# Down-projection's first 40 k-tiles by one level of Strassen's algorithm, in four chunks

## The chip, the core and the metric

The kernel runs on one core of a Trainium2 chip. Its engines run side by side and wait for each other through semaphores: TensorE (PE: matmuls into PSUM), VectorE (DVE), ScalarE (ACT), GpSimd (POOL) and SyncE (SP), whose queue issues nearly all transfers between HBM and SBUF. The metric is the device time of one execution, in microseconds.

## The reference, cut to the part that matters

One layer: token mixers, then a gated feed-forward network, then a residual and a final norm. The part at hand is the last third:

```
def conv_ffn(h, st, w_up, ffn_conv_w, ffn_conv_b, w_down):
    gate, val = jnp.split(h @ w_up, 2, axis=-1)
    gate_c, new_st = causal_dwconv(gate, st, ffn_conv_w)
    act = jax.nn.silu(gate_c + ffn_conv_b) * val
    return act @ w_down, new_st
...
        f, s_f = conv_ffn(h, ffn_s[l], w_up[l], ffn_conv_w[l], ffn_conv_b[l], w_down[l])
        x = x + g2 * f
...
    y = rmsnorm(x, final_norm)
```

There are 576 positions (512 of the prompt, 64 of the sample), 2048 model columns and 5632 hidden columns, all float32.

## The kernel before

Everything is held transposed: features on the 128 partitions, positions along the free dimension in two halves of 288 (256 prompt, 32 sample). With P = 128 the hidden size is 44 tiles (NFF), the model size 16 (KD).

Float32 precision comes from two-part operands. Each operand is split into a high part (a rounded copy, made by ScalarE) and a low part (the difference, by VectorE), and a product is three matmuls: high x high, high x low, low x high. Weights are split as they arrive (`up_split`, `wtile`), activations once.

The up stage (`up`, `up_prep`, `up_product`, `up_out`) already uses one level of Strassen's algorithm in Winograd's form. A unit is one hidden tile t. Its four weight blocks a11, a21, a22, a12 (8 k-tiles of 128 columns each) are loaded by `up_load` into six raw buffers; VectorE makes four sums of them; seven products of 8 x 3 matmuls on 290 columns follow, each against a combination of the activations that was made once and stays in SBUF (`combos[c, j]`, 7 x 8 slots). The combinations' order is B11, T1, T2, B21, T3, B22, T4. Three PSUM banks per unit gather the products. A product's weights are split two steps ahead (`ahead = 2`; three buffers each for high and low parts). The gate's convolution and the activation (`up_conv`, `up_act`) of unit t-1 are done while unit t runs, and the result goes to HBM as `actd[t]`.

The down stage (`down`) takes the hidden tiles in groups of four. `acts(g)` loads four tiles of `actd` and splits them, one group ahead. For each of the 16 output tiles, `mm6` does the six matmuls of each k-tile (three products, two halves of 288 columns), and `residual` multiplies by the gate and adds onto `x1[m]`, which was reloaded from `xd[m]`. The slots for all that are the up stage's combinations, which are no longer needed.

The last group of four k-tiles is in `final`, together with the transposition back, the final norm and the stores.

The program's text is not the order of execution: a list scheduler orders each engine's instructions by priority and by when it expects their operands. Once ordered, an engine runs its instructions in order, and so does SyncE with the transfers that it issues.

Of the kernel before, what the change touches and what calls it, by code (L numbers as in the profile page):

```python
# [16 lines left out]
P = 128  # L17
# [23 lines left out]
N_HRAW = 9  # L41
N_RAW = 6
NW = 66
OFF_AQ, OFF_AK, OFF_AV, OFF_AR, OFF_ALR = 0, 512, 1024, 2048, 3072
# [55 lines left out]
class Kern:  # L100
# [633 lines left out]
    def raw_late(self):  # L734

        pool, tag = self.raws[self.n_raw % N_RAW]
        self.n_raw += 1
        return pool.tile([P, 1024], F32, tag=tag, name=self.name("raw"))

# [767 lines left out]
    def parts(self, j):  # L1507
        lo, hi = self.x1[j], self.x1[j + NPAIR]
        return lo[:, 0], lo[:, 1], hi[:, 0], hi[:, 1]
# [96 lines left out]
    def up_load(self, t, names):  # L1606
        for n in names:
            raw = self.raw_late().rearrange("p (k n) -> p k n", k=NPAIR)
            row, half = {"a11": (0, 0), "a12": (0, 1), "a21": (1, 0), "a22": (1, 1)}[n]
            self.nc.sync.dma_start(raw, self.w_cols("w_up", row * NFF + t, half * NPAIR)(0, NPAIR))  # L1610
            self.a[t, n] = raw

    def up_split(self, src):
        hi, lo = [self.wq.tile([P, 1024], F32R, tag="w" + c, bufs=3, name=self.name("w" + c))
                  .rearrange("p (k n) -> p k n", k=NPAIR) for c in "hl"]
        self.nc.scalar.activation(hi, src, AF.Copy)  # L1616
        self.nc.vector.tensor_tensor(lo, src, hi.bitcast(F32), op=ALU.subtract)  # L1617
        self.split_of = self.nc.cur_bb.bb.instructions[-1]
        return hi, lo

    def up_s(self, c):
        return self.ua.tile([P, NPAIR, P], F32, tag=f"s{c}", name=self.name("s"))

    def up_first(self, t):

        s1 = self.a[t, "s1"] = self.up_s(1)
        self.nc.vector.tensor_tensor(s1, self.a[t, "a21"], self.a[t, "a22"], op=ALU.add)  # L1627

    def up_prep(self, t, c):

        V, a = self.nc.vector, self.a
        g = lambda n: a[t, n]
        if c == 0:
            w = self.up_split(g("a11"))
            with self.tc.issue_after(self.split_of):
                self.up_first(t)
        elif c == 1:
            w = self.up_split(g("s1"))
            s2 = a[t, "s2"] = self.up_s(2)
            with self.tc.issue_after(self.split_of):  # L1640
                V.tensor_tensor(s2, g("s1"), g("a11"), op=ALU.subtract)
        elif c == 2:
            w = self.up_split(g("s2"))
            if t + 1 < NFF:
                self.up_load(t + 1, ("a11", "a21"))
        elif c == 3:
            w = self.up_split(g("a12"))
        elif c == 4:
            V.tensor_tensor(g("a21"), g("a11"), g("a21"), op=ALU.subtract)
            w = self.up_split(g("a21"))  # L1650
            if t + 1 < NFF:
                self.up_load(t + 1, ("a22", "a12"))
        elif c == 5:
            V.tensor_tensor(g("s2"), g("a12"), g("s2"), op=ALU.subtract)
            w = self.up_split(g("s2"))
        else:
            w = self.up_split(g("a22"))
        a[t, "w", c] = w

    def up_product(self, t, c):  # L1660

        if c == 0:
            self.banks = [self.bank()[:, :HZ] for _ in range(3)]
        T, (wh, wl) = self.nc.tensor, self.a.pop((t, "w", c))
        ps = self.banks[(0, 2, 1, 0, 1, 2, 1)[c]]
        for j in range(NPAIR):
            hi, lo, _ = self.combos[c, j]

            T.matmul(ps, wh[:, j], hi, start=(c < 3 and j == 0), stop=False, skip_group_check=True)  # L1669
            T.matmul(ps, wh[:, j], lo, start=False, stop=False, skip_group_check=True)  # L1670
            T.matmul(ps, wl[:, j], hi, start=False, stop=(j == NPAIR - 1), skip_group_check=True)  # L1671

    def up_out(self, t, c):

        nc = self.nc
        V, A, G = nc.vector, nc.scalar, nc.gpsimd
        x, y, z = self.banks
        tmp = lambda n: self.ub.tile([P, HZ], F32, tag=n, name=self.name(n))
# [50 lines left out]
    def up_begin(self):  # L1729

        self.a, self.n_raw = {}, 0
        self.up_load(0, ("a11", "a21", "a22", "a12"))

    def up(self):
# [3 lines left out]
        self.up_state(0)  # L1738
        self.t2s = {}
        ahead = 2  # L1740
        steps = [(t, c) for t in range(NFF) for c in range(7)]
        for n, (t, c) in enumerate(steps):
            if t == 0:
                for l in ((1,), (2,), (3,), (4,), (5, 6), (), ())[c]:
                    for j in range(N_EARLY, NPAIR):
                        self.pair_late(l, j)
            if n + ahead < len(steps):
                self.up_prep(*steps[n + ahead])
            self.up_product(t, c)
            if n == 0:  # L1750
                norm = self.norm_end()
            if n < 2:
                next(norm, None)

            if t > 0 and c == 0:
                with self.tc.issue_after(self.split_of):
                    self.up_conv(t - 1, self.ca)
                self.up_state(t)
            if t > 0 and c == 2:
                with self.tc.issue_after(self.split_of):  # L1760
                    self.up_act(t - 1, self.v, self.ca)
            self.up_out(t, c)
        self.up_conv(t, self.ca)
        self.up_act(t, self.v, self.ca)


    def acts(self, g):

        nc, out = self.nc, []
        places = self.sets[g % 2]  # L1770
        for n in range(4):
            raw, hh, hl = [self.slot(places[3 * n + i], (F32, F32R, F32R)[i], HT) for i in range(3)]
            nc.sync.dma_start(raw, self.actd[4 * g + n])
            nc.scalar.activation(hh, raw, AF.Copy)
            nc.vector.tensor_tensor(hl, raw, hh.bitcast(F32), op=ALU.subtract)
            out.append((hh, hl))
        return out

    def down(self):
        free = [self.combos[c, j][2] for c in range(7) for j in range(NPAIR)]  # L1780
        take = lambda n: [free.pop(0) for _ in range(n)]
        self.sets = [take(12), None]
        acts = self.acts(0)
        self.raw = self.raw_late
        places = take(KD)
        self.sets[1] = take(12)
        for m in range(KD):
            self.x1[m] = self.slot(places[m], F32)
            self.nc.sync.dma_start(self.x1[m], self.xd[m])
        for g in range(NFF // 4 - 1):  # L1790
            for m0 in range(0, KD, 2):
                wh, wl = self.wtile(self.w_down(4 * g, m0))
                if m0 == 6:
                    ahead = self.acts(g + 1)
                for m in range(m0, m0 + 2):
                    ps = self.pgt()
                    c = slice((m - m0) * P, (m - m0 + 1) * P)
                    for k in range(4):
                        self.mm6(ps, wh[:, k, c], wl[:, k, c], acts[k], k == 0, k == 3)
                    self.residual(ps, self.x1[m], self.mod[:, 5, m])  # L1800
            acts = ahead
        g = NFF // 4 - 1
        self.final(acts, free + self.sets[(g + 1) % 2] + self.sets[g % 2][0::3])

# [5 lines left out]
    def final(self, acts, free):  # L1810
# [10 lines left out]
        for h in range(2):  # L1821
# [3 lines left out]
            for m in range(KD):  # L1825
# [4 lines left out]
                for k in range(4):  # L1830
                    self.mm6(ps, w[m][0][:, k], w[m][1][:, k], acts[k], k == 0, k == 3, ((h, HT),), m % 2)
                self.residual(ps[:, m % 2:m % 2 + 1], self.x1[m][:, h:h + 1], self.mod[:, 5, m])
                if late and m % 4 == LATE:
# [39 lines left out]
    def final_part(self, h, q, blocks):  # L1873
# [3 lines left out]
        for c0, n, y, ms in blocks:  # L1877
            ps = self.bank()
            z0 = c0 if c0 < HP else ZS
            for j in range(4):  # L1880
                T.transpose(ps[:n, j * P:(j + 1) * P], self.x1[4 * q + j][:, h, z0:z0 + n], self.c["ident"])
            junk = self.v_tile().rearrange("p h t -> p (h t)")
# [22 lines left out]
def layer_kernel(tc, i, o):  # L1905
    nc = tc.nc
    with ExitStack() as ctx:
# [10 lines left out]
        nc.vector.memset(K.zero3, 0.0)  # L1918
        K.xd = [dp.tile([P, 2, HZ], F32, name=f"xd{m}") for m in range(KD)]
        K.actd = [dp.tile([P, 2, HT], F32, name=f"actd{t}") for t in range(NFF)]  # L1920
        K.hp = pool(ctx, "hp", bufs=1)
        K.wq = pool(ctx, "wq", "right", bufs=3)
        with ExitStack() as early:
# [46 lines left out]
            K.norm_begin()  # L1970
            K.raws = [(K.ua, f"r{n}") for n in range(4)]
            K.up_begin()
# [12 lines left out]
        K.ub = pool(ctx, "ub", "right", bufs=1)  # L1985
        K.raws += [(K.ub, f"r{n}") for n in range(4, N_RAW)]
        K.up()
        K.down()
# [131 lines left out]
```

## Time and profile before

| what | us |
|---|---|
| median of 3 runs (2852.7 to 2855.14) | 2854.19 |
| the profiled execution | 2851.53 |
| its span, first to last instruction | 2849.8 |
| first matmul of the up stage | 1262.5 |
| first matmul of the down stage | 2264.7 |
| first matmul of the final stage | 2771.6 |

The profile's page gives each engine's busy time and a chain of waits, followed back from the last instruction. Groups of instructions are named by line, engine, operation and tiles, output first ("g<-slot,wh": into tile g from slot and wh). "Idle before" is the time for which the engine waited just before such an instruction, with what released it. Windows give busy times in a stretch of the span. A recorded duration includes some overlap with the next instruction of the same engine, so the rate of a series is read from start to start.

### The profile page before, as it was taken

To read this page: it belongs to the slowest core of one execution; us is meant where nothing else is said; L and a number is where in the kernel's file an instruction comes from. 1 tells how busy PE (TensorE), PEld (TensorE's weight loads), DVE (VectorE), ACT (ScalarE), POOL (GpSimd) and SP (SyncE) were. 2 spreads that over 40 slices of the span, in tenths; PEclk is the share of its full clock that TensorE was granted. 3 is DMA by queue.
4 is the path that set the end of the run, shared out by engine and by line. 5 is a ranking of instruction groups with operands and counts; after the bars stand their busy time and mean duration, and the time that the engine had idled before them with its cause. 6 is when DMAs were issued, how large, how long until landed. Compare 5 with 4: busy or idle time off the path is not lost.

```text
span 2849.8 us, 52385 instructions
## 1 busy us (share of the span) xinstructions
PE 2796.4 (98%) x21092; PEld 2724.1 (96%) x21092; DVE 2109.3 (74%) x3625; ACT 1193.3 (42%) x2058; POOL 186.5 (7%) x245
## 2 busy tenths in 40 slices
PE   7999999999999999999999999999999999999998
PEld 5799999999999999999999999999999999999997
DVE  4578787787877887678888888888888855555565
ACT  4255654553535442554444444444444412222123
POOL 0001000010000000000111111111111000000000
PEclk9999999999999999999999999999999999999999
DMA  9965455455554567633333333333333643333221
GB/s 307 324 198 165 135 138 146 135 171 152 154 150 125 154 189 211 179 100 113 102 103 108 103 111 110 109 102 102 109 102 112 215 152 116 103 99 117 87 76 67
DMA packets 544023, 395.56 MB, mean 139 GB/s; under 512 B 60041, under 2 KB 486276, under 8 KB 543780
## 3 DMA queue, kind: packets, MB, share of 16 engines
q1 hardware_dynamic: 536436, 390.54, 46.1%
q8 instruction: 166, 2.72, 0.4%
q10 hardware_dynamic: 7344, 1.67, 0.3%
q14 instruction: 77, 0.63, 0.1%
HBM read 356.47 MB, written 35.67 MB: 138 GB/s over the span
## 4 chain that ended last, share of the span: by engine, by line
PE 84%; DVE 7%; issue 3%; DMA 3%; ACT 2%; POOL 1%; SPq 0%; ACTq 0%; DVEq 0%; POOLq 0%
PE g L643 28%; PE g L645 14%; PE bank L1670 12%; PE bank L1669 11%; PE bank L1671 11%; PE bank L2042 4%; DVE acc L2026 2%; PE bank L2038 1%; PE bank L865 1%; DVE wl L2026 1%; DVE m L2002 1%; DMA d<-m 0%; DMA hs<-in_x_prompt_dram 0%; DVE ca L2026 0%; DMA cm<-d 0%
## 5 line engine op out<-in xcount | busy, mean ns | idle before, releaser
L1670 PE MATMUL bank<-slot,wh 128*128 128x290 f32 x2464 | 737.6, 299 | 0.0
L1669 PE MATMUL bank<-slot,wh 128*128 128x290 f32 x2464 | 733.9, 298 | 1.4 <-ACT sqa L1594 1.2
L1671 PE MATMUL bank<-slot,wl 128*128 128x290 f32 x2464 | 728.8, 296 | 0.0
L643 PE MATMUL g<-slot,wh 128*128 128x288 f32 x3168 | 550.5, 295 | 0.2 <-DVE slot L2026 0.2
L643 PE MATMUL g<-hh,wh 128*128 128x288 f32 x2048 | 473.8, 312 | 1.9 <-ACT ts L2026 1.7
L1671 PEld LDWEIGHTS bank<-slot,wl 128*128 128x128 f32 x2464 | 470.9, 191 | 0.0
L1670 PEld LDWEIGHTS bank<-slot,wh 128*128 128x128 f32 x2464 | 468.4, 190 | 0.1
L1669 PEld LDWEIGHTS bank<-slot,wh 128*128 128x128 f32 x2464 | 463.4, 188 | 1.9 <-ACT sqa L1594 1.4
L643 PEld LDWEIGHTS g<-slot,wh 128*128 128x128 f32 x3168 | 463.0, 188 | 0.7 <-DVE slot L2026 0.5
L2026 ACT ACTIVATE wh<-raw 128x1024 fp32r<-128x1024 f32 x215 | 227.6, 1058 | 547.7 <-PE g L643 533.4
L645 PE MATMUL g<-hh,wl 128*128 128x288 f32 x2048 | 442.2, 297 | 1.7 <-DVE wl L1023 1.7
L643 PE MATMUL g<-hl,wh 128*128 128x288 f32 x2048 | 442.5, 297 | 0.0
L2026 DVE SCALAR_TENSOR_TENSOR slot<-g,mod,slot 128x512 f32<-128x512 f32 (+1 forms) x448 | 201.7, 491 | 261.9 <-PE g L645 256.4
L643 PEld LDWEIGHTS g<-hh,wh 128*128 128x128 f32 x2048 | 325.8, 190 | 22.6 <-issue 15.1
L645 PE MATMUL g<-slot,wl 128*128 128x288 f32 x1584 | 340.9, 294 | 0.0
L645 PEld LDWEIGHTS g<-hh,wl 128*128 128x128 f32 x2048 | 330.8, 189 | 5.1 <-issue 3.1
L643 PEld LDWEIGHTS g<-hl,wh 128*128 128x128 f32 x2048 | 330.8, 189 | 3.3 <-issue 2.4
L2026 DVE TENSOR_TENSOR wl<-raw,wh 128x1024 fp32r<-128x1024 f32 x215 | 261.6, 1217 | 47.0 <-ACT wh L2026 44.6
L1616 ACT ACTIVATE wh<-raw 128x1024 fp32r<-128x1024 f32 x176 | 186.0, 1057 | 221.9 <-PE bank L1670 184.5
L1617 DVE TENSOR_TENSOR wl<-raw,wh 128x1024 fp32r<-128x1024 f32 x176 | 215.3, 1223 | 54.3 <-ACT wh L1616 54.3
L645 PEld LDWEIGHTS g<-slot,wl 128*128 128x128 f32 x1584 | 255.3, 188 | 0.0
L1616 ACT ACTIVATE wh<-s 128x1024 fp32r<-128x1024 f32 x132 | 140.1, 1062 | 210.5 <-DVE s L1627 109.5
(320 smaller groups left out, 3231.2 us busy)
## 6 DMA issues: line engine op xcount, KB each, us to landing
raw<-in_w_up_dram SPq DMA_DIRECT2D x176, 512.0 KB
raw<-in_w_in_dram SPq DMA_DIRECT2D x100, 512.0 KB
raw<-in_w_down_dram SPq DMA_DIRECT2D x88, 512.0 KB
aw<-in_w_ada_dram SPq DMA_DIRECT2D x79, 512.0 KB
xr<-in_w_ada_dram SPq DMA_DIRECT2D x49, 512.0 KB
hraw<-in_w_ada_dram SPq DMA_DIRECT2D x40, 512.0 KB
raw<-in_w_out_dram SPq DMA_DIRECT2D x32, 512.0 KB
slot<-actd SPq DMA_DIRECT2D x44, 288.0 KB
```

The source lines that it names most:

```text
L643: T.matmul(ps[:, h if bank is None else bank, :n], wh, x[:, h, :n], start=f, stop=False)
L645: T.matmul(ps[:, h if bank is None else bank, :n], wl, ah[:, h, :n], start=False, stop=stop)
L865: T.matmul(ps[32 * k:32 * k + 32, :w], cs[:, k0 + k], got[n][k // per][:, k % per], start=(k0 == 0), stop=(k0 == KD - 4))
L1616: self.nc.scalar.activation(hi, src, AF.Copy)
L1617: self.nc.vector.tensor_tensor(lo, src, hi.bitcast(F32), op=ALU.subtract)
L1669: T.matmul(ps, wh[:, j], hi, start=(c < 3 and j == 0), stop=False, skip_group_check=True)
L1670: T.matmul(ps, wh[:, j], lo, start=False, stop=False, skip_group_check=True)
L1671: T.matmul(ps, wl[:, j], hi, start=False, stop=(j == NPAIR - 1), skip_group_check=True)
L2002: return f(*a, **kw)
L2026: return f(*a, **kw)
L2038: return self.engine.transpose(out, *a)
L2042: return self.engine.matmul(out, *a, **kw)
```

## The change

The first 40 hidden tiles of the down-projection are done like the up stage: one level of Strassen's algorithm, over pairs of k-tiles (even and odd), pairs of output tiles (u and u + 8) and the two halves of the positions. There are four chunks (NCH) of five pairs (NJ). A chunk has eight units, one for each u; a unit has seven products of 5 x 3 matmuls on 288 columns. The units follow the up stage's 44 in the same list of steps (N_UNITS = 44 + 32). Product 6 of a unit is put off until after product 0 of the next (`DOWN_ORDER`).

The activations' seven combinations per pair are made in the up stage. `pair_put` loads two finished tiles of `actd`, GpSimd makes the four sums and the low parts, ScalarE the high parts, and the 14 results go to HBM (`cd`). It is a generator whose pieces run at steps 2, 3, 5 and 6 of the even units and 0, 2, 3 and 5 of the odd ones. In the down stage `fill` loads each combination of a chunk into a slot of its own, 35 for a chunk, as slots come free: those of the up stage for the first chunk; for the later ones those that the last unit of the chunk before frees, product by product, and six spare ones.

`down_out` moves each product from PSUM onto the accumulators `x1` (in the first chunk ScalarE copies where there is nothing to add to). In the last chunk GpSimd adds the shared first product (`sums`), and `down_end` multiplies by the gate on ScalarE and adds the residual, loaded from `xd`, on GpSimd. Weight blocks are 5 x 128 columns, loaded in runs of 512 bytes by the extended `up_load`, with four more raw buffers. The final stage keeps its four k-tiles; `x1` has 288 columns per half there in place of 290.

```
+NJ, NCH = 5, 4
+N_UNITS = NFF + KD // 2 * NCH
+DOWN_ORDER = (0, 6, 2, 1, 3, 4, 5)
...
@@ up_load
+                g, m = divmod(t - NFF, NPAIR)
+                m += row * NPAIR
+                raw = raw[:, :NJ]
+                w = self.i["w_down"][0, 2 * NJ * g * P:2 * NJ * (g + 1) * P, m * P:(m + 1) * P]
+                self.nc.sync.dma_start(raw, w.rearrange("(j s p) n -> s p j n", s=2, p=P)[half])
...
+    def down_prep(self, t, c):
+        V, a = self.nc.vector, self.a
+        g = lambda n: a[t, n]
+        if c == 0:
+            w = self.up_split(g("a11"))
+            with self.tc.issue_after(self.split_of):
+                self.up_first(t)
+                s2 = a[t, "s2"] = self.up_s(t, 2)
+                V.tensor_tensor(s2, g("s1"), g("a11"), op=ALU.subtract)
...
+        elif c == 2:
+            w = self.up_split(g("s2"))
+            if t + 1 < N_UNITS:
+                self.up_load(t + 1, ("a22", "a12"))
+        elif c == 3:
+            w = self.up_split(g("a12"))
+            if t + 2 < N_UNITS:
+                self.up_load(t + 2, ("a11", "a21"))
...
@@ up_product
-        for j in range(NPAIR):
-            hi, lo, _ = self.combos[c, j]
+        n = NPAIR if t < NFF else NJ
+        for j in range(n):
+            hi, lo, _ = self.combos[c, j] if t < NFF else self.dn[(t - NFF) // NPAIR, c, j]
...
@@ up
+        for t in range(NFF, N_UNITS):
+            steps += [(t, c) if c < 6 else (t - 1, c) for c in DOWN_ORDER if c < 6 or t > NFF]
+        steps.append((N_UNITS - 1, 6))
...
+            if (t, c) == (NFF - 1, 0):
+                self.raws[0:0] = [(self.xp, f"j{n}") for n in range(4)]
+                self.vacant += [(self.xp, f"j{n}") for n in (4, 5)]
+                self.want(0)
...
+    def pair_put(self, p):
+        nc, cd = self.nc, self.cd[p]
+        A, G = nc.scalar, nc.gpsimd
+        tiles = lambda dt, *ns: [self.xp.tile([P, 2, HT], dt, tag=f"j{n}", name=self.name("j")) for n in ns]
+        (r0, r1), (ta, tb) = tiles(F32, 0, 1), tiles(F32, 2, 3)
+        for s, r in enumerate((r0, r1)):
+            nc.sync.dma_start(r, self.actd[2 * p + s])
+        yield
+        G.tensor_tensor(ta[:, 0], r0[:, 1], r0[:, 0], op=ALU.subtract)
+        G.tensor_tensor(tb[:, 0], r1[:, 1], r0[:, 1], op=ALU.subtract)
+        G.tensor_tensor(ta[:, 1], r1[:, 1], ta[:, 0], op=ALU.subtract)
+        G.tensor_tensor(tb[:, 1], r1[:, 0], ta[:, 1], op=ALU.subtract)
+        for parts in (((ta, slice(0, 2), slice(T1, T2 + 1)), (tb, slice(0, 2), slice(T3, T4 + 1, 2))),
+                      ((r0, slice(0, 1), slice(B11, B11 + 1)), (r1, slice(0, 2), slice(B21, B22 + 1, 2)))):
+            yield
+            his = tiles(F32R, 4, 5)
+            for (src, k, _), hi in zip(parts, his):
+                A.activation(hi[:, k], src[:, k], AF.Copy)
+            yield
+            for (src, k, _), hi in zip(parts, his):
+                G.tensor_tensor(src[:, k].bitcast(F32R), src[:, k], hi[:, k].bitcast(F32), op=ALU.subtract)
+            yield
+            for (src, k, c), hi in zip(parts, his):
+                nc.sync.dma_start(cd[:, c, 0], hi[:, k].bitcast(F32))
+                nc.sync.dma_start(cd[:, c, 1], src[:, k])
...
+    def want(self, g):
+        self.pending += [(g, c, j) for c in (0, 2, 1, 3, 4, 5, 6) for j in range(NJ)]
...
+    def fill(self):
+        while self.pending and self.vacant:
+            g, c, j = self.pending.pop(0)
+            place = self.vacant.pop(0)
+            t = self.slot(place, F32, HT)
+            self.nc.sync.dma_start(t, self.cd[g * NJ + j][:, c])
+            self.dn[g, c, j] = t[:, 0].bitcast(F32R), t[:, 1].bitcast(F32R), place
...
+    def down_out(self, t, c):
+        g, u = divmod(t - NFF, NPAIR)
+        x, y, z = self.a[t, "banks"]
...
+        lo, hi, p = self.x1[u], self.x1[u + NPAIR], self.sums[u]
+        ps, dst, new = ((x, p, True), (z, hi[:, 1], True), (y, lo[:, 1], True), (x, lo[:, 0], True),
+                        (y, hi[:, 1], False), (z, lo[:, 1], False), (y, hi[:, 0], True))[c]
+        if g == 0 and new:
+            A.activation(dst, ps, AF.Copy)
+        else:
+            V.tensor_tensor(dst, ps, dst, op=ALU.add)
+        if u == NPAIR - 1:
+            if c == 0 and g + 1 < NCH:
+                self.want(g + 1)
+            self.vacant += [self.dn.pop((g, c, j))[2] for j in range(NJ)]
+            self.fill()
+        if g == NCH - 1:
+            if c == 1:
+                self.down_end()
...
+            elif c == 6:
+                G.tensor_tensor(lo[:, 1], lo[:, 1], p, op=ALU.add)
+                G.tensor_tensor(hi, hi, p.unsqueeze(1).to_broadcast([P, 2, HT]), op=ALU.add)
+                self.ended.append((u, self.xt))
...
+    def down_end(self):
+        while self.ended:
+            u, xt = self.ended.pop(0)
+            for n, x in enumerate(xt):
+                m = u + n * NPAIR
+                for s, q, f in ((slice(0, HP), slice(0, HP), 0), (slice(HP, HT), slice(ZS, HZ), 1)):
+                    d = self.x1[m][:, :, s]
+                    nc.scalar.activation(d, d, AF.Copy, scale=self.mod[:, 5, m, f:f + 1])
+                    nc.gpsimd.tensor_tensor(d, d, x[:, :, q], op=ALU.add)
...
     def down(self):
...
-        for g in range(NFF // 4 - 1):
-            for m0 in range(0, KD, 2):
-                wh, wl = self.wtile(self.w_down(4 * g, m0))
...
+        self.down_end()
         self.raw = self.raw_late
-        places = take(KD)
...
+        self.raws = [r for r in self.raws if r[0] is not self.xp]
+        self.final(self.last_acts, self.vacant)
```

154 lines of the change are left out of this document (102 added, 52 removed).

## The prediction

> **What bounds the kernel now.** I read the page first, then the stage windows, then the waits inside the stages that the change touches.
>
> ```profile
> span 2849.8 us, 52385 instructions
> PE 2796.4 (98%) x21092; PEld 2724.1 (96%) x21092; DVE 2109.3 (74%) x3625; ACT 1193.3 (42%) x2058; POOL 186.5 (7%) x245
> PE 84%; DVE 7%; issue 3%; DMA 3%; ACT 2%; POOL 1%; SPq 0%; ACTq 0%; DVEq 0%; POOLq 0%
> ```
>
> TensorE carries the chain. The stage windows say how tightly; the columns are the window, its length, each engine's busy time with its instruction count, granted clock, DMA share and GB/s.
>
> ```profile
> core 0: us, PE busy (x) PEld busy (x) DVE busy (x) ACT busy (x) POOL busy (x), PEclk, DMA share, GB/s
> 2264.70:2771.60 506.90, 506.90 (x3843) 506.89 (x3842) 275.91 (x452) 115.14 (x129) 0.00 (x0) 1.00 0.36 115
> 1307.50:2215.10 907.60, 907.60 (x6723) 907.60 (x6722) 751.91 (x921) 405.87 (x480) 99.49 (x120) 1.00 0.37 107
> ```
>
> The first row is the down-projection over its first 40 k-tiles. 16 output tiles x 40 k-tiles x 6 matmuls are 3840, so one costs 506.9/3840 = 132.0 ns, with no TensorE idle. The second row is 40 units of the up stage (already Strassen): 40 x 7 x 24 = 6720 matmuls, 135.06 ns each, a unit 22.69 us, again no idle. So a matmul removed in down is worth its full price, any new wait there costs its full length, and the up stage can only lose.
>
> **The change part by part.**
>
> *Removed: products.* Four chunks x 8 units x 7 products x 15 matmuls are 3360 in place of 3840, 480 fewer. The new order (high x high, high x low, low x high into one bank) already runs in the final stage on 288 columns:
>
> ```profile
> 2772.53 0.43 PE L643 MATMUL g<-slot,wh 128*128 128x288 f32 x2
> ...
> 2774.77 0.29 PE L645 MATMUL g<-slot,wl 128*128 128x288 f32 x1
> ```
>
> Seventeen matmuls start from 2772.53 up to 2774.77: 2.24/17 = 131.8 ns. I take 132.0: 3360 x 0.132 = 443.5 us, a gain of 63.4. The other end is the up stage's 135.06 ns (same loop, but 290 columns): 453.8 us, a gain of 53.1. The final row is nearer, having the width and the order.
>
> *Added: VectorE work in down.* A unit needs 7 splits, 4 weight sums and 7 evictions, at 640 and 288 columns.
>
> ```profile
> L1023 DVE TENSOR_TENSOR wl<-raw,wh 128x512 fp32r<-128x512 f32 x9 | 6.1, 685 | 0.0
> L1023 DVE TENSOR_TENSOR wl<-raw,wh 128x768 fp32r<-128x768 f32 x6 | 5.7, 950 | 0.0
> L1694 DVE TENSOR_TENSOR g<-bank,g 128x290 f32<-128x290 f32 x44 | 19.9, 453 | 1.0 <-PE bank L1671 1.0
> 1901.71 1.22 DVE L1641 TENSOR_TENSOR s<-s,raw 128x1024 f32<-128x1024 f32 x1
> 1902.84 0.46 DVE L1699 TENSOR_TENSOR v<-bank,p 128x290 f32<-128x290 f32 x1
> ```
>
> 640 columns interpolate to 0.82 us. The last two rows show that a recorded time overlaps the next start by 0.09 (1.13 from start to start for 1.22), so I count 0.73 and 0.37. 11 x 0.73 + 7 x 0.37 = 10.6 us, against a unit of 7 x 15 x 0.132 = 13.86. Splits run two steps (3.96 us) ahead and the worst step (split, two sums, one eviction: 2.6 us) fits under that. Price nothing, cover 3.3 us per unit; without it the excess would go to TensorE 32 times. ScalarE's 7 splits are shorter and it was busy 115 of 507 us.
>
> *Added: reloading 35 combination tiles per chunk.* This is the main cost. Loads share one queue:
>
> ```profile
> 2265.00:2290.00 25.00, 25.00 (x193) 25.00 (x192) 16.73 (x28) 7.44 (x10) 0.00 (x0) 1.00 1.02 336
> GB/s 378 377 348 359 381 384 325 361 131 173 359 345 355 350 335 348 363 344 345 354 369 338 342 383 352 348 375 393 289 140 339 382 343 269 133 178 343 311 311 336
> q1 hardware_dynamic: 7694, 9.70, 98.8%
> slot<-actd SPq DMA_DIRECT2D x44, 288.0 KB
> 2761.09 3.35 DMA raw<-in_w_down_dram
> ```
>
> The saturated stretch (share 1.02) moves 336 GB/s, its slices (2265 to 2295) mostly 340 to 380; practically all of it is queue q1. A combination tile is 288 KB, as the activation row: 294,912 B / 336 = 0.878 us; 35 of them 30.7. A lone 512 KB load on the chain took 3.35 us, of which 1.56 is moving at 336, so a latency of 1.79. Weights in 512-byte runs move as in the up stage (107 GB/s at share 0.37, so 289): 1.31 MB per unit are 4.53 us.
>
> A slot comes free only when its product of the chunk's last unit is done. Count from that unit's start, a step 1.98 us. After step 0 eleven tiles can be asked for (5 freed, 6 spare), then five after each of steps 2 to 6. The next chunk's first unit needs them from step 7 on; the last five (product 6) at step 15, 29.7 us. The 35th lands at 1.98 + 1.79 + 30.7 + 6/7 x 4.53 of weights queued between = 38.4: late by 8.7. The three inner boundaries cost 26 us. At 380 GB/s it is 5.1 each (15); with one more unit of weights in front 13.2 each (40).
>
> At the first boundary the up stage's combinations free slots during its last unit, ten after its first product (3.24 us), all 35 by its fifth. With the weights of one and a half units queued between they land at 3.24 + 1.79 + 30.7 + 1.5 x 4.53 = 42.5, needed at 22.69 + 7 x 1.98 = 36.6: 6 us late (2 at 380 GB/s, 10 with another unit of weights). Sum of boundaries: 32 us, between 17 and 50. What is late next is only the weights behind those tiles, and the raw buffers reach 2.5 units ahead.
>
> *Added to the up stage: GpSimd and ScalarE make the combinations.* Each of 20 pairs, over two units (45.4 us), has 8 GpSimd subtractions, 4 x 288 + 3 x 576 + 288 = 3168 columns. The nearest rows are a one-input GpSimd operation on 512 columns, alone and beside VectorE:
>
> ```profile
> 725.17 1.24 POOL L2056 TENSOR_SCALAR_AFFINE_SELECT m<-m 128x512 f32<-128x512 f32 x2 [24.85 <-ACT m L2002]
> 275.18 1.68 POOL L2056 TENSOR_SCALAR_AFFINE_SELECT m<-m 128x512 f32<-128x512 f32 x2 [19.88 <-ACT m L2002]
> 275.18 2.22 DVE L2026 SCALAR_TENSOR_TENSOR acc<-xr,ct,acc 128x512 f32<-128x512 f32 x2
> 316.39 2.73 DVE L2026 SCALAR_TENSOR_TENSOR acc<-aw,ct,acc 128x512 f32<-128x512 f32 x4
> ```
>
> Two take 1.24 us alone and 1.68 in collision. Four VectorE operations undisturbed take 2.73, starting 0.66 apart, so two take 1.41; in collision 2.22. VectorE lost 0.81 us to 1024 GpSimd columns, 0.79 ns each: they take turns. A second input has to be read too: I double it to 1.58, so 5.0 us of VectorE per pair; the ends are 0.79 (2.5) and twice the whole time alone (2 x 1.21 = 2.42 ns, 7.7). VectorE's idle time in the 40 units:
>
> ```profile
> DVE wl L1617 <- ACT wh L1616: 71.6, 162, 0.6
> DVE v L1692 <- PE bank L1671: 42.2, 40, 1.1
> DVE g L1689 <- PE bank L1671: 40.3, 40, 1.0
> ```
>
> 154.1 us, 7.7 per pair: the 5.0 fit. Locally:
>
> ```profile
> 1907.86 1.22 DVE L1617 TENSOR_TENSOR wl<-raw,wh 128x1024 fp32r<-128x1024 f32 x1
> 1914.90 0.46 DVE L1689 TENSOR_TENSOR g<-bank,sqa 128x290 f32<-128x290 f32 x1 [1.00 <-PE bank L1671]
> ```
>
> The low half for product 3 is ready at 1909.08. That product ends at 1914.90 and lasts 24 x 0.135, so it starts at 1911.66: 2.6 us of slack. The burst of four subtractions costs VectorE 1152 x 1.58 = 1.8 us (2.8 at the end of the range). I take 5 us for the stage, 0.25 per pair; ends 0 and 48 (below, the second rival). A gain is excluded, TensorE having no idle there.
>
> The Trainium skill, page "SBUF — State Buffer", section "Who interferes with whom", states that a VectorE instruction with two SBUF inputs and a GpSimd instruction that reads SBUF exclude each other for a whole instruction; the trace agrees, 2.22 us for 1.41. The page "GPSIMD Engine Reference", section 3.1, gives 4497 ns for an add of 2048 columns; the estimate by it is 2.2 ns a column, 7.0 us per pair, still under the idle time, and the sum would not move.
>
> ScalarE's added copies are under 3 us per pair with the engine busy 405.87 of 907.60. The queue carries 20 x (0.59 read + 2.06 written) = 53 MB more, 58 GB/s on 107. Both hidden. SyncE's queue gets two loads and eight stores per pair ahead of weight loads; these wait for a GpSimd or ScalarE result, and what stands behind them is the next unit's weights, already prefetched.
>
> *Last chunk and end.* GpSimd adds 288 + 576 + 2 x 576 = 2016 columns per unit: 3.2 us of VectorE (4.9 at the end), on 10.6 of 13.86. 2.6 of the 10.6 read PSUM and may run beside. I take 3 us in all, between 0 and 13. The last two tiles' adds are wanted seven output tiles into the final stage, 7 x 12 x 0.132 = 11 us later: hidden. The final four k-tiles keep their instructions.
>
> **Sum.** The profiled run took 2851.53 (span 2849.8). 2851.5 - 63.4 + 32 + 5 + 3 = 2828.1. The median of the runs before is 2854.19, 2.7 above that run, so 2831.
>
> **Rivals.**
> 1. *The transfers keep up*, chance 0.18. For it: slices at 380 GB/s, and weights that could be fetched before the boundary. Against: 10.3 MB per boundary in 26 us is 397 GB/s by itself. With boundaries at 8 us in all, 2807; with none, 2799.
> 2. *GpSimd takes VectorE's slack away*, chance 0.20; slower. Place: the up stage, units 3 to 42. From 2.42 ns a column on the idle time (7.7 per pair) is gone and every further microsecond is TensorE's; at 3.2 ns a pair needs 10.1, 2.4 us x 20 = 48, giving 2831 - 5 + 48 = 2874. It ends slower than before from 2.9 ns on. For it: 83% VectorE in the window and bursts against 2.6 us of slack. Against: the doubled row leaves a third of the idle time.
> 3. *A queue blocks*, chance 0.10: ScalarE's copies of the combinations stand in order before weight splits and wait for GpSimd; or SyncE's stores hold the weight loads. 2 us per pair beyond the slack is 40 us: 2866. Against: a split is needed some 4 us after ScalarE does it.
> 4. *The products aren't cheaper as counted*, chance 0.05: at 135 ns each and with the boundaries at their upper end, 2851.5 - 53.1 + 50 + 8 + 2.7 = 2859.
>
> **How the numbers follow.** My forecast has 0.47, its own range 2808 to 2852 (boundaries 17 to 50, price of a matmul, the small terms). The range for 8 in 10 reaches into rivals 1 and 2: 2794 to 2880. A measurement tells 0.2% (5.7 us) from nothing. Faster: rival 1 (0.18) and 0.43 of the forecast's 0.47, 0.61 with a little of the others; slower: most of 2, 3 and part of 4, 0.30; the rest, 0.09, within 0.2%.
>
> **What would show it.** A TensorE count lower by 480; near 132 ns per matmul inside a down unit; TensorE idle only at four places, 6 to 9 us each, released by a transfer into a combination slot, with the DMA share at 1.0 there; the up stage still near 22.7 us per unit with VectorE's idle time mostly gone. Up units longer by over 1 us, with TensorE waiting for a low half, would make rival 2 right; boundaries without a wait, rival 1.

## The result and the profile after

The changed kernel takes 2897.25 us (median of 4 runs, 2889.95 to 2899.74), the kernel before 2854.66 in the same comparison: a ratio of 1.0144, 95% interval 1.0122 to 1.0165. It is slower by 1.4%; 2831 was forecast, in a range up to 2880. Two runs below, one of e6 (9987.88 us) and one of the kernel before beside it (9591.86), took over three times as long as all others and are left out.

The page of the kernel after: the span, the engines' busy time, the chain, and the matmul group with the largest wait.

```profile
span 2898.0 us, 52822 instructions
PE 2777.0 (96%) x20612; PEld 2676.8 (92%) x20612; DVE 2277.3 (79%) x3721; ACT 1308.3 (45%) x2314; POOL 455.6 (16%) x453
PE 40%; issue 21%; DVE 19%; DMA 9%; ACT 5%; POOL 5%; SPq 0%; ACTq 0%; DVEq 0%; POOLq 0%
L1724 PE MATMUL bank<-slot,wl 128*128 128x290 f32 (+1 forms) x3024 | 902.0, 298 | 52.2 <-DVE wl L1629 52.1
```

There are 480 matmuls fewer (21092 to 20612), as counted. But TensorE, whose share of the chain was 84%, has 40%, and the low-part matmul now waits for a low part that VectorE makes. Windows of the kernel after (stretch, length, busy time of each engine with its count, clock, DMA share, GB/s): the up stage, then chunk 1 and chunk 4 of down.

```profile
1310.00:2340.00 1030.00, 976.99 (x7058) 958.14 (x7057) 862.01 (x968) 462.51 (x584) 316.53 (x286) 1.00 0.52 156
...
2345.00:2457.00 112.00, 112.00 (x841) 111.31 (x840) 77.86 (x109) 54.15 (x97) 0.05 (x1) 1.00 0.59 182
...
2683.70:2816.40 132.70, 120.47 (x842) 115.33 (x841) 108.84 (x151) 57.51 (x94) 52.75 (x42) 0.97 0.55 164
```

Two stretches have idle TensorE: the up stage (53 us of 1030) and the last chunk. Chunk 1 has none. Both that suffer have a busy GpSimd. Taking the first matmul of each stage from the traces gives the balance (spans 2849.8 and 2898.0):

```
                               before    after   difference   forecast
up stage                       1002.2   1079.7     +77.5         +5
down: 3360 for 3840 products    507       449      -58          -63.4
down: three inner boundaries      -         3       +3          +26
down: boundary after up           -         0        0           +6
down: last chunk over chunk 1     -        20      +20           +3
before the up stage            1262.5   1265.1      +2.6          0
final stage to the end           78.2     81.6      +3.4          0
```

(449 is 3360 times chunk 1's 112.2/840 = 133.5 ns; the last chunk is 132.7 in place of 112.2, and 1 us of that is its boundary's. Units and chunks of down are counted in runs of 105 and 840 matmuls from 2344.75; as product 6 is put off, a run after the first begins one product, 2 us, after its unit's product 0.) The time before the up stage, where nothing changed, moves by a few microseconds from run to run: 1264.3 to 1270.2 in the runs below.

The up stage's loss is in the odd units alone. From first matmul to first matmul an even unit takes 22.69 us, as before; an odd one (3 to 41) 26.54 on average. The odd units are where a pair's work falls. One such unit begins at 1878.76. VectorE, ScalarE and GpSimd around its start, from the timeline of each:

```profile
1873.44 1.22 DVE L1629 TENSOR_TENSOR wl<-raw,wh 128x1024 fp32r<-128x1024 f32 x1 [0.50 <-ACT wh L1628]
...
1877.48 1.05 DVE L1748 TENSOR_TENSOR g<-g,sqa 128x290 f32<-128x290 f32 x1
1880.91 2.29 DVE L1629 TENSOR_TENSOR wl<-s,wh 128x1024 fp32r<-128x1024 f32 x1 [2.37 <-ACT wh L1628]
1883.12 1.82 DVE L1656 TENSOR_TENSOR s<-s,raw 128x1024 f32<-128x1024 f32 x1
...
1885.34 1.76 DVE L1753 TENSOR_TENSOR v<-v,sqa 128x580 f32<-128x580 f32 x1
```

```profile
1872.35 1.06 ACT L1628 ACTIVATE wh<-raw 128x1024 fp32r<-128x1024 f32 x1 [2.18 <-PE bank L1723]
1878.25 0.69 ACT L1866 ACTIVATE j<-j 128x576 fp32r<-128x576 f32 x1 [4.84 <-POOL j L1859]
1879.24 0.68 ACT L1866 ACTIVATE j<-j 128x576 fp32r<-128x576 f32 x1 [0.30 <-POOL j L1860]
1879.83 1.04 ACT L1628 ACTIVATE wh<-s 128x1024 fp32r<-128x1024 f32 x1
```

```profile
1875.63 0.85 POOL L1858 TENSOR_TENSOR j<-j,j 128x288 f32<-128x288 f32 x1 [11.56 <-DMA j<-actd]
1876.43 1.79 POOL L1859 TENSOR_TENSOR j<-j,j 128x288 f32<-128x288 f32 x1
1878.30 0.91 POOL L1860 TENSOR_TENSOR j<-j,j 128x288 f32<-128x288 f32 x1
1879.29 4.57 POOL L1869 TENSOR_TENSOR j<-j,j 128x576 fp32r<-128x576 f32 x3
```

Two things go wrong in the same ten microseconds. First, ScalarE's copy of a combination (L1866) stands in its order before the split `wh<-s` and waits 4.84 us for GpSimd, which itself had waited for the load of the second tile. The split starts at 1879.83; in the next, even unit (start 1905.03) the same split starts at 1902.19, 2.84 before the unit, so here it is 3.9 us late. Second, VectorE's operations are longer where GpSimd reads: 2.29 for 1.23, 1.82 for 1.22, 1.76 for 0.77, 1.05 for 0.46. That is 3.2 us in four operations. The slack was 2.6.

What GpSimd cost VectorE over the whole stage shows in VectorE's busy time over units 2 to 41, where it has the same 922 instructions in both kernels (windows, before and after, from the first matmul of unit 2 to that of unit 42):

```profile
1311.88:2219.34 907.46, 907.46 (x6722) 907.46 (x6721) 751.77 (x922) 405.90 (x481) 99.53 (x121) 1.00 0.37 107
...
1314.74:2299.38 984.64, 931.63 (x6723) 912.78 (x6721) 824.11 (x922) 442.81 (x562) 310.77 (x280) 1.00 0.52 154
```

VectorE is busy 72.3 us longer: about 3.6 us for each of the 20 pairs, 1.1 ns for each of a pair's 3168 columns.

In the last chunk the same pair of lines shows, from the waits:

```profile
ACT slot L1938 <- POOL slot L1924: 19.8, 7, 3.3
...
ACT slot L1938 <- POOL slot L1923: 15.4, 8, 3.3
```

ScalarE's scaling of the finished tiles (L1938) waits 35.2 us in all for GpSimd's adds, with weight splits behind it. Part of the loss there is TensorE's granted clock, the share of full speed at which it is let run (the third column from the end of a window): in two stretches it is half, and the matmuls stand 0.24 us apart in place of 0.13. The first of them:

```profile
2772.70:2776.00 3.30, 3.30 (x16) 3.30 (x16) 2.00 (x4) 0.74 (x1) 0.00 (x0) 0.51 0.73 224
```

The two cost 3 us of the 20. The up stage has two such stretches as well (3 us of its 77.5). All four follow waits of TensorE, but most of the up stage's waits, as long as these, are not followed by one; what decides it is open.

The end of the last chunk reaches into the final stage. There a copy stands in VectorE's order before an eviction, waits for GpSimd's last adds (L1939), and TensorE waits for the eviction (VectorE's, then TensorE's timeline):

```profile
2822.11 0.29 DVE L2027 COPY v<-bank 88x128 f32<-88x128 f32 x1 [2.73 <-POOL slot L1939]
```

```profile
2823.00 0.53 PE L646 MATMUL g<-slot,wh 128*128 128x288 f32 x2 [2.48 <-DVE slot L1988]
```

With 1 us at half the granted clock behind it, that accounts for the final stage's +3.4.

### The profile page after: what moved, and what is told of

It reads as the page before. It is cut to its first block, busy times and chain, and to the rows that moved or that the text cites. A ratio compares the mean times of both kernels' runs of the same rounds, so it can differ in the third digit from the quotient of the medians.

```text
span 2898.0 us, 52822 instructions
## 1 busy us (share of the span) xinstructions
PE 2777.0 (96%) x20612; PEld 2676.8 (92%) x20612; DVE 2277.3 (79%) x3721; ACT 1308.3 (45%) x2314; POOL 455.6 (16%) x453
## 3 DMA queue, kind: packets, MB, share of 16 engines
q10 hardware_dynamic: 7344, 1.67, 0.3%
## 4 chain that ended last, share of the span: by engine, by line
PE 40%; issue 21%; DVE 19%; DMA 9%; ACT 5%; POOL 5%; SPq 0%; ACTq 0%; DVEq 0%; POOLq 0%
PE g L646 17%; PE g L648 8%; DVE wl L1629 5%; PE bank L2200 4%; DMA actd<-v 4%; PE bank L1724 2%; PE bank L1722 2%; PE bank L1723 2%; DVE ca L1772 2%; ACT wh L1628 2%; DMA j<-actd 2%; DVE acc L2184 2%; DVE s L1656 2%; PE bank L2196 1%; PE bank L868 1%
## 5 line engine op out<-in xcount | busy, mean ns | idle before, releaser
L1724 PE MATMUL bank<-slot,wl 128*128 128x290 f32 (+1 forms) x3024 | 902.0, 298 | 52.2 <-DVE wl L1629 52.1
L1722 PE MATMUL bank<-slot,wh 128*128 128x290 f32 (+1 forms) x3024 | 903.8, 299 | 4.5 <-ACT wh L1628 3.3
L1723 PE MATMUL bank<-slot,wh 128*128 128x290 f32 (+1 forms) x3024 | 904.1, 299 | 0.0
L1722 PEld LDWEIGHTS bank<-slot,wh 128*128 128x128 f32 x3024 | 569.9, 188 | 10.8 <-ACT wh L1628 4.9
L1723 PEld LDWEIGHTS bank<-slot,wh 128*128 128x128 f32 x3024 | 574.9, 190 | 0.1
L1628 ACT ACTIVATE wh<-raw 128x1024 fp32r<-128x1024 f32 (+1 forms) x304 | 279.9, 921 | 328.4 <-PE bank L1723 236.3
L1629 DVE TENSOR_TENSOR wl<-raw,wh 128x1024 fp32r<-128x1024 f32 (+1 forms) x304 | 322.8, 1062 | 93.4 <-ACT wh L1628 90.5
L1629 DVE TENSOR_TENSOR wl<-s,wh 128x1024 fp32r<-128x1024 f32 (+1 forms) x228 | 271.7, 1193 | 70.5 <-ACT wh L1628 69.8
L1628 ACT ACTIVATE wh<-s 128x1024 fp32r<-128x1024 f32 (+1 forms) x228 | 209.7, 921 | 205.4 <-PE bank L1723 74.5
L2184 ACT ACTIVATE wh<-raw 128x1024 fp32r<-128x1024 f32 x135 | 142.7, 1058 | 205.9 <-PE g L646 195.7
L2184 DVE TENSOR_TENSOR wl<-raw,wh 128x1024 fp32r<-128x1024 f32 x135 | 165.0, 1223 | 44.7 <-ACT wh L2184 42.0
L1722 PE MATMUL g<-slot,wh 128*128 128x288 f32 x560 | 169.4, 303 | 9.0 <-DVE slot L1907 7.1
L1723 PE MATMUL g<-slot,wh 128*128 128x288 f32 x560 | 166.9, 298 | 0.0
```

What stands on the lines that cost most here:

```text
L1724: T.matmul(ps, wl[:, j], hi, start=False, stop=(j == n - 1), skip_group_check=True)
L2184: return f(*a, **kw)
```

## The experiments

Two theories. W: the wait in ScalarE's order; its copies wait for GpSimd in front of weight splits. P: the port; VectorE and GpSimd exclude each other when both read SBUF. The odd units tell them apart (before: 22.69, after: 26.54).

### Copies behind the split (e1)

```
         self.nc.scalar.activation(hi, src, AF.Copy)
+        self.split_act = self.nc.cur_bb.bb.instructions[-1]
...
-                A.activation(hi[:, k], src[:, k], AF.Copy)
+                with self.tc.issue_after(self.split_act):
+                    A.activation(hi[:, k], src[:, k], AF.Copy)
```

> Same work; in the up stage ScalarE's copies of the combinations are put in ScalarE's order behind the weight split of the step to which they belong. Theory W (ScalarE's copies wait for GpSimd in front of weight splits): odd up units fall from 26.4 to between 22.7 and 23.7 us, the run to 2820 to 2845. Theory P (GpSimd's reads of SBUF hold VectorE up): odd units stay at 26 us or more, the run at 2885 or more.

Odd units 24.36 us (24.17 to 24.59); the run 2855.45 us, ratio to the kernel before 0.9998 (0.9989 to 1.0008). Neither theory alone: the order was worth 2.2 us of the 3.85, and 1.67 are left. TensorE's waits in the up stage of e1, then VectorE's and GpSimd's timeline at the place:

```profile
PE bank L1723 <- DVE g L1741: 28.6, 20, 1.7
```

```profile
1917.93 3.28 DVE L1780 SCALAR_TENSOR_TENSOR v<-v,ca 128x512 f32<-128x512 f32 x2
1921.14 0.45 DVE L1741 TENSOR_TENSOR g<-bank,p 128x290 f32<-128x290 f32 x1
```

```profile
1917.47 3.66 POOL L1871 TENSOR_TENSOR j<-j,j 128x576 fp32r<-128x576 f32 x2 [1.30 <-ACT j L1868]
```

The two VectorE operations take 3.28 us where they took 0.94 before: two GpSimd operations of 576 columns have cost VectorE 2.34 us, 1.17 each, 2.0 ns a column at this place. The eviction behind them (L1741) is late, and TensorE waits for its bank, once in each of the 20 odd units. Over units 2 to 41 the price is lower, as the window shows:

```profile
1320.12:2261.00 940.88, 912.26 (x6723) 908.02 (x6721) 855.79 (x922) 443.32 (x560) 351.01 (x278) 1.00 0.53 159
```

VectorE is busy 104.0 us longer than before: 5.2 us per pair, 1.6 ns a column. The edit took away the waits and let GpSimd meet VectorE more often (3.6 us per pair in the kernel after), so the 2.2 us that the order was worth are what is left after that.

### GpSimd reads two columns (e2)

```
+        G.memset(ta[:, 0], 0.0)
-        G.tensor_tensor(ta[:, 0], r0[:, 1], r0[:, 0], op=ALU.subtract)
+        G.tensor_tensor(ta[:, 0, :2], r0[:, 1, :2], r0[:, 0, :2], op=ALU.subtract)
...
```

> Leaves out the arithmetic of the combinations: each GpSimd subtraction of the up stage reads 2 columns in place of 288 or 576 (the sums' tiles are filled by a memset, which reads nothing). ScalarE's copies, their order and their wait for the load and for GpSimd stay. W: the copies still wait about 4 us in place of 4.8 ahead of a split, odd units 25 to 26 us. P: odd units 22.7 to 23.2 us.

Odd units 23.07 us on average, 13 of 20 at 22.69, as P said; the run 2828.54 us (one run). VectorE's busy time over units 2 to 41 is 749.3 us, as before (751.8), although GpSimd still fills the sums' tiles by a memset: it is GpSimd's reading that makes VectorE's operations longer. ScalarE's wait for GpSimd was still there, but shorter, as its waits in the up stage show:

```profile
ACT j L1870 <- POOL j L1862: 51.3, 19, 4.0
```

2.7 us a time in place of the 5.0 of the kernel after (99.7 us in 20 waits), and nearly all of it fits into the slack. W's number (25 to 26) is missed: the wait alone, at this length, costs little.

### Copies by GpSimd (e3)

```
-                A.activation(hi[:, k], src[:, k], AF.Copy)
+                G.tensor_copy(hi[:, k], src[:, k])
```

> The high parts of the combinations are copied by GpSimd in place of ScalarE: nothing of ScalarE waits for GpSimd any more, and GpSimd reads 2016 columns more per pair. W: odd units 22.7 to 24 us. P: odd units 27 us or more.

Odd units 26.98 us, the run 2910.39 (one run). With nothing of ScalarE waiting any more, more GpSimd reading makes it as bad as before: VectorE is busy 129 us longer than in the kernel before. P's number, all but 0.02, but in part by the clock: in twelve stretches of this up stage the granted clock is 0.50, which is 19 of the 86 us that the odd units lose. Without them they would take about 26.0 us, still far above W's 24.

### Scaling behind the split in the last chunk (e4)

```
-                    nc.scalar.activation(d, d, AF.Copy, scale=self.mod[:, 5, m, f:f + 1])
+                    with self.tc.issue_after(self.split_act):
+                        nc.scalar.activation(d, d, AF.Copy, scale=self.mod[:, 5, m, f:f + 1])
```

> Same work; only in the last chunk of down ScalarE's scaling of the finished tiles is put behind the weight split of its step. W: the last chunk falls from 132.7 us by 10 to 18, the up stage unchanged. P: by 0 to 3.

The last chunk takes 123.5 us in place of 132.7: 9 less, nearly half of its excess over chunk 1 (112.2); the run 2889.93 (one run). Just under W's range; the rest stays.

### VectorE makes the combinations, order free (e9) and behind the split (e5)

e9 is the first edit alone; e5 is e1 with the second.

```
-        G.tensor_tensor(ta[:, 0], r0[:, 1], r0[:, 0], op=ALU.subtract)
+        V.tensor_tensor(ta[:, 0], r0[:, 1], r0[:, 0], op=ALU.subtract)
...
```

```
+        with self.tc.issue_after(self.split_of):
+            V.tensor_tensor(ta[:, 0], r0[:, 1], r0[:, 0], op=ALU.subtract)
...
```

> Only GpSimd's eight subtractions moved to VectorE, ScalarE's copies left where the scheduler puts them. W alone (ScalarE still waits for the late load in front of weight splits): odd units 24 to 26 us. P alone: 22.7 to 23.1 us.

> As e1, but VectorE makes the combinations' sums and low parts, in its order behind the weight split's low half; GpSimd reads nothing large in the up stage. By start-to-start times (0.37 us for 288 columns, 0.66 for 576) that is 3.8 us of VectorE per pair, out of 7.7 idle. P (what e1 left over is VectorE held up by GpSimd's reads): odd units 22.7 to 23.1 us, the run 2815 to 2828. If instead the work as such is too much for the slack: odd units stay above 24 us.

e9: odd units 23.92 us (23.05 to 26.55), just under W's range, the run 2847.62. e5: every unit 22.69, as P said, the run 2823.43 (one run each). So the port is not enough by itself either; with it gone, the free order still costs 1.2 us per odd unit. Two rows of e9's waits show whose order: ScalarE's copies wait, now for VectorE, and VectorE's own subtraction waits for the load, both in front of weight splits:

```profile
ACT j L1866 <- DVE j L1859: 71.8, 19, 6.4
...
DVE j L1858 <- DMA j<-actd: 64.3, 19, 6.0
```

The four cases of the up stage's odd units ("behind the split" holds for VectorE's subtractions too):

```
                        order free     behind the split
GpSimd subtracts          26.54                24.36
VectorE subtracts         23.92                22.69
```

Each theory explains a part, both eat the same slack of some 3 us, and together they cost more (3.85) than the sum of the two single cases (1.67 + 1.23 = 2.90). The 1.23 are those of two engines' order; what ScalarE's alone costs without GpSimd was not run.

e5 moves all that the kernel after moves and keeps ScalarE's copies and SyncE's stores, and its up stage loses nothing:

```profile
1317.62:2225.08 907.46, 907.46 (x6722) 907.46 (x6721) 819.67 (x1079) 448.27 (x559) 121.58 (x121) 1.00 0.56 165
```

So the added transfers (165 GB/s for 107 before) cost nothing by themselves. The window also tells why VectorE does better with more work. Its own eight operations add 67.9 us to its busy time, 3.4 us per pair; in e1, where the same eight are GpSimd's and the copies stand behind the split too, VectorE loses 5.2 us per pair.

### The last chunk: order only (e6), and on VectorE (e7)

e6 is e5 with e4's edit. e7 is e5 with:

```
-                G.tensor_tensor(lo[:, 1], lo[:, 1], p, op=ALU.add)
-                G.tensor_tensor(hi, hi, p.unsqueeze(1).to_broadcast([P, 2, HT]), op=ALU.add)
+                with self.tc.issue_after(self.split_of):
+                    V.tensor_tensor(lo[:, 1], lo[:, 1], p, op=ALU.add)
+                    V.tensor_tensor(hi, hi, p.unsqueeze(1).to_broadcast([P, 2, HT]), op=ALU.add)
...
-                    nc.scalar.activation(d, d, AF.Copy, scale=self.mod[:, 5, m, f:f + 1])
-                    nc.gpsimd.tensor_tensor(d, d, x[:, :, q], op=ALU.add)
+                    with self.tc.issue_after(self.split_of):
+                        nc.vector.scalar_tensor_tensor(d, d, self.mod[:, 5, m, f:f + 1], x[:, :, q],
+                                                       op0=ALU.mult, op1=ALU.add)
```

> e5 and, in the last chunk, ScalarE's scaling behind the weight split as in e4. W and P: the last chunk near 123 us as in e4, the run 9 to 10 us under e5: 2806 to 2820, faster than before by 1.2 to 1.7%.

> e5 and, in the last chunk, VectorE in place of GpSimd for the shared product, and one VectorE operation (multiply, add) in place of ScalarE's scaling and GpSimd's add. VectorE then has 10.6 + 2.8 us of a 13.9 us unit. P: the last chunk 112 to 117 us, the run 2798 to 2812. If VectorE's time is too short: 120 us or more, above e6.

e6: 2814.21 us (median of 3), ratio 0.9853 (0.9832 to 0.9874); its last chunk takes 123.1 us. Both are as expected. e7: 2806.77, ratio 0.9827 (0.9811 to 0.9842). Its windows, up stage, last chunk and a stretch in the last chunk's last unit:

```profile
1310.00:2260.00 950.00, 950.00 (x7038) 950.00 (x7037) 857.91 (x1126) 468.35 (x583) 126.58 (x126) 1.00 0.57 167
...
2609.10:2727.90 118.80, 115.36 (x844) 113.48 (x842) 110.96 (x191) 47.45 (x66) 0.00 (x0) 0.99 0.60 183
...
2720.60:2724.20 3.60, 3.60 (x17) 3.60 (x18) 2.07 (x4) 1.14 (x2) 0.00 (x0) 0.57 0.92 281
```

The up stage is full again, 950.00 of 950.00. The last chunk is 118.8, between the two ranges named: units with the finished tiles' adds 14.3 us, fine; its second unit (16.4) and its last (18.0) carry most of what is left. In the second, TensorE waits 1.2 us for an eviction, beside the boundary's 1 us; in the last it waits 1.8 us for a low part, and the granted clock is half for the 3.4 us that follow, which is another 1.4.

### The boundaries (e10, e11, e12)

The forecast had 8.7 us at each inner boundary and the trace shows about 1. In the order of SyncE's transfers in the kernel after, before the run of chunk 2 begins at 2456.9, and in the window of the same stretch:

```profile
2441.55 21.07 SPq L1884 DMA_DIRECT2D slot<-cd  x29
2463.04 13.89 SPq L1621 DMA_DIRECT2D raw<-in_w_down_dram  x10
```

```profile
2441.50:2462.50 21.00, 21.00 (x158) 20.83 (x158) 14.71 (x22) 9.35 (x17) 0.00 (x0) 1.00 0.98 362
```

29 tiles are issued in a row, at 0.73 us each, not one weight load between; the other six had gone out a chunk earlier, from 2364.85 on, because the scheduler did not wait for the last unit to use the spare slots. Three terms differ from the forecast; the runs take them away one at a time, on top of e7.

```
e10, e12:
-                self.vacant += [(self.xp, f"j{n}") for n in (4, 5)]
...
-                    self.vacant += [(self.ub, n) for n in ("g", "ca", "cb")]
e11, e12:
-                self.raws[0:0] = [(self.xp, f"j{n}") for n in range(4)]
```

> e7 with five of the six spare slots taken away, so that a later chunk's combinations can hardly be loaded before the last unit of the chunk before. If the six tiles loaded a chunk ahead are what hides the boundaries: the first two units of chunks 2, 3 and 4 together grow by 2 to 5 us each time. If the transfers' rate alone is enough (29 tiles went out in 21 us): by under 1 us.

> e7 without the four extra raw buffers, so weights are at most 1.5 units ahead and their loads fall between the combinations'. If the depth of the weights is what keeps the boundaries short: the first two units of chunks 2, 3 and 4 grow by 3 to 6 us each time. If not: by under 1 us.

> e7 with both changes, which is nearest to what the prediction priced at 8.7 us per inner boundary. If its three terms (rate, no early tiles, weights between) were each too high only together: 3 to 8 us per boundary. If the rate alone decides: under 2 us.

First two units of each later chunk together (two ordinary units are 13.93 + 14.12 = 28.05 us; the excess is that of chunks 2 and 3, since chunk 4 has its own work), and one run of each:

```
                           chunk 2   chunk 3   chunk 4   over 28.05     run
e7                          29.03     29.04     30.30       1.0       2806.77 (median)
e10, one spare slot         30.56     30.51     32.91       2.5       2817.01
e11, six raw buffers        35.60     35.74     35.57       7.6       2827.95
e12, both                   36.60     36.57     36.77       8.5       2832.71
```

In chunks 2 and 3, e10's growth of 1.5 us lies between its two forecasts, e11's 6.6 above "3 to 6", e12's 7.5 in "3 to 8". What is late differs. In e11 TensorE waits, once at each of the two boundaries, for a weight's high part: with six buffers the weights come behind the tiles. Then the granted clock is half and some twenty matmuls stand 0.24 us apart, which is some 2.4 of the 7.6 us (TensorE's waits from 2270 to 2600, and the window of one such stretch):

```profile
PE g L1723 <- ACT wh L1628: 6.2, 2, 3.1
```

```profile
2401.00:2407.20 6.20, 6.20 (x25) 6.08 (x26) 4.26 (x6) 1.91 (x3) 0.00 (x0) 0.50 0.73 231
```

In e12's waits of TensorE it is the tiles, as foreseen:

```profile
PE bank L1723 <- DMA slot<-cd: 7.1, 10, 2.2
```

With both taken away the boundary costs 8.5 us, against 8.7 worked out before. That it is so close is in part luck: among e12's 35 tiles at chunk 2 stand eight weight loads, where the sum had 3.4; the longest row of tiles goes out at 0.74 us each (17 in 12.62), not 0.878; and 1.4 of the 8.5 us are matmuls at half the granted clock.

What made the boundary short is the depth of the weights' buffers (6.6 us by itself) and, for less, the early tiles (1.5); the transfers' rate, which e12 leaves as it was, does not do it alone.

## Why the prediction was wrong

*The products.* 3360 at 133.5 ns, not 132.0: a gain of 58 in place of 63.4, inside the bounds named (53.1 to 63.4). The mechanism is right, the size a little off: in chunk 1 most products run at 131.6 to 134.3 ns a matmul, and one in fourteen at 147. Why that one does was not followed.

*VectorE's and ScalarE's work in down.* Right: chunk 1 shows no wait of TensorE (112.00 of 112.00).

*The transfers, stores and copies added to the up stage.* Right as far as their amount goes: e5 keeps them all and loses nothing.

*The boundaries.* Forecast 32, found 3. The step that failed is the weights that were put "queued between": with ten buffers they had all been loaded, and the queue held nothing but tiles. The text itself said that the buffers reach 2.5 units ahead, and did not draw the conclusion. e11 and e12 show it. The boundary after the up stage, put at 6, costs nothing in the kernel after and 2.5 in e12 (30.53 for the first two units of chunk 1).

*The up stage.* This is the step that decided: "I take 5 us for the stage", found 77.5. A sum that was about right was held against the wrong slack, and an order was left out.
- The price was not the error. 1.58 ns of VectorE for a GpSimd column, from a doubled one-input row, made 5.0 us per pair; VectorE lost 3.6 in the kernel after and 5.2 in e1 (1.1 and 1.6 ns). At the place shown for e1 it was 2.0. The Trainium skill's estimate of 2.2 ("GPSIMD Engine Reference", section 3.1: 4497 ns for 2048 columns on GpSimd itself) lies above all of these. By the mean idle time, 7.7 us per pair, all of them fit.
- The mean idle time failed. The 7.7 us are spread over two units, while seven of a pair's eight subtractions fall into the eleven microseconds from 1875.63 on, at the odd unit's start, where VectorE had next to no idle time: in the kernel before, around the unit that starts at 1901.7, its timeline shows a single wait, of 0.29 us, from 1896.42 to 1911.74. The slack there was 2.6 us, and it was compared with the burst of four subtractions alone; the low parts, which follow at once, were left out. e1, with the order mended, still loses 1.67 us per odd unit to it.
- The order failed. ScalarE's copies were priced by their length ("under 3 us per pair", "hidden"), and their wait only as rival 3, at a chance of 0.10. The diff places them at step 2 of the odd unit, and I read the time of execution from that; the scheduler had moved them in front of the split of the unit's step 1. That was 2.2 of the 3.85 us. SyncE's stores, the other half of that rival, cost nothing (e5).

*The last chunk.* Forecast 3, upper end 13, found 20: the same two causes. e4 takes away 9 by the order, e7 another 5; half the granted clock is 3 of the 20.

*The end.* The last tiles' adds were called hidden because TensorE needs them late. VectorE came to wait for them earlier, and the final stage is 3.4 us longer.

*The rivals.* Rival 2 named the right place (the odd units' burst against 2.6 us) and the sign, and its 2874 is nearest of all, but partly by luck: it needs 3.2 ns a column and a threshold by mean idle time of 2.42, where 1.1 to 1.6 and a bad order were enough. Rival 3 was the other half, and the two were taken as alternatives although both draw on one slack. Rival 1 (transfers keep up) came true beside them. Against the sum, the up stage and the last chunk lost 90 us, the products 5, the stages before and behind 6, and the boundaries gained 29: two large errors met, and the total looks less wrong than its terms.

What stays open: the second and the last unit of the last chunk in e7 still take 2.3 and 3.8 us more than ordinary ones, and no run was made on the waits that show there. Nor was one made on the load for which GpSimd waits 11.56 us before a pair's work: beginning the pair's work later was not tried.

## What to carry to other kernels

Moving elementwise work off a busy VectorE onto GpSimd can cost VectorE more than doing it: here 5.2 us a pair against 3.4, because operations with two SBUF inputs take turns with GpSimd's reads. Compare a burst with the slack at the place where it lands, not with the mean idle time of the stage, and let all that draws on one slack draw together. Where a scheduler orders the engines, an instruction that waits for a slow producer is to be pinned behind the work of the critical path; one such edge on ScalarE's order was worth 2.2 us in each of 20 units. After a change that makes TensorE wait, look at the granted clock too: the matmuls behind a wait can run at half of it.

## What the runs showed of the hardware

Loads of 2304-byte runs alone in the queue moved at more than the 336 GB/s of the 25 us of mixed loads before: 362 over the 21 us shown above, and 407 in ten of them.

```profile
2450.00:2460.00 10.00, 10.00 (x76) 9.83 (x76) 7.95 (x13) 4.29 (x7) 0.00 (x0) 1.00 1.05 407
```

A VectorE operation of 64 columns can last until a GpSimd operation of 576 columns is done: in e1's two timelines above VectorE's pair ends at 1921.21, GpSimd's at 1921.13. The groups of one line by shape, first in the kernel after, then in e1's up stage (where the line is one further down):

```profile
L1779 DVE SCALAR_TENSOR_TENSOR v<-v,ca 128x64 f32<-128x64 f32 x44 | 12.3, 279 | 0.0
```

```profile
L1780 DVE SCALAR_TENSOR_TENSOR v<-v,ca 128x64 f32<-128x64 f32 x41 | 57.9, 1411 | 0.0
```

With the copies in another place of ScalarE's order, GpSimd's next work meets another operation of VectorE: the same 64 columns take 279 ns in the one kernel and 1411 in the other.

The Trainium skill's rule that the other "fully blocks" (page "SBUF — State Buffer", section "SBUF: two separate sides") agrees with e1's row: 1411 ns is five times the operation's own time.

After some waits TensorE's granted clock is 0.50 for a while, and a matmul of 288 columns then follows the last one after 0.24 us in place of 0.13: 25 in the 6.2 us of e11's window above.
